# Turning rows in 64-row tiles into pairs of PSUM banks, with the order inside a step written out

## The chip, the cores and the metric

The kernel runs on one core of one Trainium2 chip. The metric is device time of one execution in microseconds. A profile of one execution comes with it: a record of each instruction's start and duration on each engine. The engines are called PE (TensorE, matrix multiply; PEld is its weight load), DVE (VectorE), ACT (ScalarE), POOL (GpSimd) and SP (SyncE, which here only issues DMA transfers). PE writes only to PSUM, a memory of eight banks, each of 512 fp32 values per partition. POOL does not read PSUM here, so what PE writes is taken out by ACT and DVE.

## The reference

Two sequences, of 2048 and 512 rows with 1024 channels, go through the same two layers and a last norm. The change lies in the second layer, Fourier mixing:

```
def fourier_layer(x, g, w_gate, w_out):
    h = rmsnorm(x, g)
    hg = h.astype(jnp.float32).reshape(b, s, N_FGROUPS, FGROUP_CH)
    f = jnp.fft.fftn(hg, axes=(1, 3), norm="ortho").real
    f = f.reshape(b, s, d).astype(x.dtype)
    gate = h @ w_gate
    return x + (f * jax.nn.silu(gate)) @ w_out
```

After it follows `rmsnorm(x, final_norm)`. In words: a transform over channels (in four groups of 256) and over positions, times a SiLU gate, times the output weights, added to the residual, normed.

## The kernel before, in words

All products are done in about fp32 precision from three matmuls each. A value is split into a high part (an ACT copy into the fp32r type) and a low part (a DVE subtraction), and `matmul3` (line 94) multiplies high by high, high by low and low by high. So each operand costs one ACT and one DVE instruction beside the PE work.

The attention layer comes first. It ends about two thirds into the span and is not changed. It already turns 64 rows at a time (line 564): the scores are turned by halves `h` into two banks, `ps[0]` and `ps[1]`, alternating `h` from turn to turn.

The Fourier layer transforms channels and computes gates first (class `Pair`, `gates`). Then come the position transforms. The transform over 2048 positions is split into 16 residues: radix-4 sums on DVE form one or two inputs `g` for each residue `k1`, and `position` multiplies them by a 128x128 cosine and sine table. For each half `hf` of the channels, `A` (cosine part, names `Ap`) and `B` (sine part, names `Bp`) are accumulated by 6 matmuls each. `B` of both halves of one position lies in the two halves of one bank. ACT copies `A` to `u` (lines 1387, 1390), DVE combines it with `B` (lines 1391 to 1394) to the rows `k1` and `16 - k1`, which gives two tiles of 128 rows, and multiplies each by its gate `s2` (line 1397).

The rows of `u` must be turned before the output product, as the channel must lie on the partitions. There are two ways through:

- `step` (residues 0 and 8, then 4, then 2): `position` for new tiles, then `finish` for an older one (48 matmuls into `fo`, the residual added at line 1425, the final norm in `normed`), then the turns of the new tiles in `split_T` (line 1000, 8 turns of 128x128 for each tile, into a new bank for each half), then `finish` of the other older tile. Between the steps DVE makes the inputs of the later residues (lines 1217, 1684 to 1708).
- `Outs` (residues 6, 1, 7, 3, 5): the products of two mirrored tiles share work by sums of their halves. `turn` (line 1442) turns half a tile into a bank, `own` makes the high and low part of a half, `sums` builds the four sums `F` and their parts `S`, and `products` runs seven products of 12 matmuls: `W` with `A[0,0]`, `Z` with `S[1]`, `W` with `S[2]`, `Z` with `S[4]`, `X` with `A[0,1]`, `W` with `S[3]`, `W` with `A[1,1]`. The position transform of the next residue is hooked in between them (`split_g`, `transform`, `turns`), and so are its turns. At the end of `products` the two finished tiles are normed and stored, each by `normed`.

The order of instructions on an engine is chosen by a scheduler when the program is built. It goes by the program's order, by what each instruction needs and by a model of durations. A helper `after(ins, anchor)` adds an edge that only fixes issue order, and `seq(engine, ins)` chains instructions of an engine with such edges. Before the change this is used in the Fourier layer only in few places (the scaling of a norm behind the last combination of `u`, line 1409).

PSUM in this part: three banks `acc` for product accumulators (`psum2`), five banks `bank` (`psum3`) in rotation for `A`, `B` and the turns.

## Time and profile before

| What | Value |
|---|---|
| Runs | 1581.34, 1581.65, 1581.80 us; median 1581.65 us |
| Profiled execution | 1581.36 us, its span 1579.4 us |
| PE busy | 1569.1 us (99%) |
| DVE busy | 1152.7 us (73%) |
| ACT busy | 876.9 us (56%) |
| POOL busy | 446.1 us (28%) |
| TensorE clock granted | 0.999 |

The page's first part lists the busy time of each engine. Matmuls are pipelined: the record of one lasts longer than the distance to the next, so rows of PE overlap, and what a group costs is read from the starts of its neighbours. In the timeline a row is a run of like instructions, with its start, the time from its start to its end, the engine, the line, the output and input names and the count; what ended an idle time before it stands in brackets. A stage view gives, for a stretch of the span, its length and then busy time and number of instructions of PE, PEld, DVE, ACT and POOL. The chain view follows the work that ended last back in time.

### The profile page before, as it was taken

The page shows a single profiled execution, that of the slowest core. Times are in us where ns is not written, and L with a number is a line of the kernel's source. Part 1 is how long each engine was busy: PE and PEld are TensorE (multiplying, and loading weights), DVE is VectorE, ACT ScalarE, POOL GpSimd, SP SyncE. Part 2 cuts the span into 40 slices and gives each one's busy share as a digit, 9 for nine tenths or more (in the row PEclk, how much of TensorE's full clock was granted, in tenths as well). Part 3 has the DMA queues.
Part 4 walks back from the last instruction along what each step waited for, and adds up shares of the span by engine and source line. Part 5 has one row for each costly group of instructions (what it writes and reads, how often), then busy time and mean ns, then how long its engine had stood idle before and what let it go on. Part 6 is the DMA issues. An engine that isn't in the chain of part 4 may idle for free.

```text
span 1579.4 us, 27487 instructions
## 1 busy us (share of the span) xinstructions
PE 1569.1 (99%) x9754; PEld 1321.5 (84%) x9754; DVE 1152.7 (73%) x2793; ACT 876.9 (56%) x2096; POOL 446.1 (28%) x614
## 2 busy tenths in 40 slices
PE   9999999999999999999999999999999999999998
PEld 7888888888888888988888888888888888888886
DVE  6888656877547786378764577669878877989796
ACT  7788535776246784167752476646655554343242
POOL 2575642421404314024222242223112111010110
PEclk9999999999999999999999999999999999999999
DMA  8587695575856567665649556675557569557762
GB/s 302 200 332 283 226 360 210 207 257 202 295 209 222 204 235 272 223 208 220 257 161 334 211 212 227 246 251 204 203 202 259 177 219 407 181 182 299 280 208 80
DMA packets 100996, 373.89 MB, mean 237 GB/s; under 512 B 11267, under 2 KB 22283, under 8 KB 83452
## 3 DMA queue, kind: packets, MB, share of 16 engines
q1 hardware_dynamic: 83148, 298.17, 53.4%
q0 software_dynamic: 16400, 70.04, 11.5%
q10 hardware_dynamic: 1312, 3.94, 0.6%
q8 instruction: 77, 1.26, 0.3%
q14 instruction: 59, 0.48, 0.1%
HBM read 280.84 MB, written 91.26 MB: 236 GB/s over the span
## 4 chain that ended last, share of the span: by engine, by line
PE 95%; DVE 3%; DMA 1%; ACT 1%; issue 1%; POOL 0%; SPq 0%; POOLq 0%; ACTq 0%; DVEq 0%
PE gp L94 14%; PE qp L94 14%; PE spt L94 11%; PE op L94 7%; PE av L590 6%; PE W L94 6%; PE spt L505 6%; PE fo L94 5%; PE vp L94 3%; PE Wo L94 3%; PE Z L94 3%; PE pt L564 3%; PE z L94 2%; PE Zo L94 2%; PE X L94 2%; PE z L1112 1%
## 5 line engine op out<-in xcount | busy, mean ns | idle before, releaser
L94 PE MATMUL gp<-h,wg 128*128 128x512 f32 x960 | 237.8, 396 | 0.0
L94 PE MATMUL qp<-h,wq 128*128 128x512 f32 x960 | 236.9, 395 | 0.0
L524 DVE CUSTOM_DVE_ANT_0 S<-spt,b 128x385 f32<-128x385 f32 (+1 forms) x320 | 156.5, 527 | 105.2 <-PE spt L505 68.0
L94 PEld LDWEIGHTS gp<-h,wg 128*128 128x128 f32 x960 | 174.9, 188 | 37.3 <-issue 1.0
L94 PEld LDWEIGHTS qp<-h,wq 128*128 128x128 f32 x960 | 174.9, 188 | 36.3 <-issue 0.2
L532 ACT ACTIVATE S<-S 128x385 f32<-128x385 f32 (+1 forms) x320 | 188.8, 597 | 19.6 <-DVE S L524 19.3
L572 ACT CAST pts<-pt 128x384 fp32r<-128x384 f32 (+1 forms) x240 | 100.4, 458 | 165.6 <-PE pt L564 156.3
L573 DVE TENSOR_TENSOR pts<-pt,pts 128x384 fp32r<-128x384 f32 (+1 forms) x240 | 114.2, 519 | 23.9 <-ACT pts L572 22.9
L94 PE MATMUL spt<-wo,uT 128*128 128x512 f32 x480 | 120.4, 391 | 0.0
L614 POOL TENSOR_TENSOR uT<-o,uT 128x256 fp32r<-128x256 f32 x75 | 55.5, 740 | 229.6 <-ACT uT L613 224.9
L94 PE MATMUL op<-wo,uT 128*128 128x512 f32 x480 | 118.9, 391 | 0.0
L505 PE MATMUL spt<-kwin,qab 64*128 64x384 f32 (+1 forms) x960 | 118.9, 353 | 0.0
L590 PEld LDWEIGHTS av<-pts,v 128*128 128x128 f32 x576 | 101.4, 188 | 18.8
L94 PE MATMUL fo<-wo,tTu 128*128 128x512 f32 x480 | 115.8, 392 | 0.2 <-ACT wo L1624 0.2
L590 PE MATMUL av<-pts,v 128*128 128x512 f32 (+1 forms) x576 | 115.7, 341 | 0.0
L94 PEld LDWEIGHTS op<-wo,uT 128*128 128x128 f32 x480 | 89.3, 188 | 18.6
L94 PEld LDWEIGHTS spt<-wo,uT 128*128 128x128 f32 x480 | 89.1, 188 | 18.3
L94 PEld LDWEIGHTS fo<-wo,tTu 128*128 128x128 f32 x480 | 88.2, 188 | 17.5 <-ACT wo L1624 0.6
L544 DVE TENSOR_SCALAR S<-S 128x384 f32<-128x384 f32 (+1 forms) x192 | 95.8, 499 | 6.8
L505 PEld LDWEIGHTS spt<-kwin,qab 64*128 64x128 f32 x960 | 74.7, 186 | 28.3 <-issue 26.1
L610 POOL TENSOR_TENSOR o<-o,s 128x256 f32<-128x256 f32 x75 | 55.3, 737 | 134.9 <-DVE o L608 134.5
L564 PEld LDWEIGHTS pt<-ident,S 64*128 64x128 f32 x1328 | 78.4, 138 | 4.2 <-issue 2.1
(333 smaller groups left out, 3195.5 us busy)
## 6 DMA issues: line engine op xcount, KB each, us to landing
wo<-wsd SPq DMA_DIRECT2D x32, 1024.0 KB, 5.2
wq<-wsd SPq DMA_DIRECT2D x31, 1024.0 KB, 7.3
wg<-wsd SPq DMA_DIRECT2D x31, 1024.0 KB, 5.6
x<-x1d SPq DMA_DIRECT2D x40, 512.0 KB, 3.6
b<-b21d SPq DMA_DIRECT2D x40, 512.0 KB, 5.8
b<-rowd SPq DMA_DIRECT2D x40, 384.0 KB, 4.3
xs<-in_x_dram SPq DMA_DIRECT2D x23, 512.0 KB, 6.9
s2d<-gt POOLq DMA_DIRECT2D x40, 256.0 KB, 5.0
```

The costliest lines, as they stand in the source:

```text
L94: pe(PE.matmul(out, a[i], b[j], start=start and i + j == 0, stop=stop and i == 1, skip_group_check=more))
L505: pe(PE.matmul(banks[j][:, 2 + k0 * P : 2 + k1 * P], res["q"][rows, qp, b * P : (b + 1) * P], kwin[g][rows, kp, b * P + k0 * P : b * P + k ...
L524: seq(DVE, DVE.tensor_tensor_reduce(out=s[:, e0:e1], in0=ps[:, 1 + e0 : 1 + e1], in1=st["bias"][:, j, 386 - e1 : 386 - e0][:, ::-1], scale ...
L532: last_exp[0] = seq(ACT, ACT.activation(s[:, e0:e1], s[:, e0:e1], AF.Exp, bias=s[:, 386:387], scale=-1.0, accum_out=s[:, 387:388]))
L544: seq(DVE, DVE.tensor_scalar(s[:, ks], s[:, ks], den, None, ALU.mult))
L564: pe(PE.transpose(ps[h][:, kb, j, :], ss[j][rows, 1 + kb * P : 1 + (kb + 1) * P], ident[rows, rows]))
L572: seq(ACT, ACT.copy(hi, ps[:, k0:k1]))
L573: seq(DVE, DVE.tensor_tensor(lo, ps[:, k0:k1], f32(hi), ALU.subtract))
L590: pe(PE.matmul(to, v, pt, start=n == part == 0, stop=part == 1 and n in (1, len(todo) - 1), skip_group_check=n > 1,))
L610: eng.tensor_tensor(o, o, s, ALU.mult)
L614: low = eng.tensor_tensor(lo, o, f32(hi), ALU.subtract)
L1112: PE.matmul(to, m[part][:, g * P : (g + 1) * P], ch[:, 0, :, odd * P : (odd + 1) * P], start=part == 0, stop=part == 1,)
```

## The change

1. Behind the step for residues 0 and 8 the pool of five banks is closed. A pool with one bank (`one`, for `B`) and a pool with two pairs of banks (`two`) take its place. `A` of one half takes the first bank of a pair, and so do the two accumulators `Vo` at the end of the last products.
2. From then on `half_turns` turns a tile. For each of its 8 blocks of 128 channels it issues two turns of 64 rows, the rows 0 to 63 into the first bank of a pair and the rows 64 to 127 into the second. One pair holds a whole tile. Two tiles take 32 turns in place of 16, chained behind the matmuls of `B` and behind each other. Readers see the pair through a view that puts the halves together again; the mirrored tile is reversed over halves and rows.
3. `step` uses `turned` in place of `split_T`: the same ACT copies and DVE subtractions, half by half over both tiles. The next `finish` starts behind the last turn.
4. `Outs`: `turns` issues all 32 turns at once. `operands` then makes the parts of the first half, sums 1, 2, 3, the parts of sums 1 and 2, and sum 4; `others`, called later, the parts of sum 4, of the two remaining halves and of sum 3. These ACT and DVE instructions are chained in that order.
5. Orders within the products are written out. `Z` with `S[4]` is cut into three quarters behind `A` and the last quarter behind `B`; `X` follows it; the adding of `X` follows the gates; `W` with `S[3]` runs two quarters, then the turns, then the other two. The norm of the first tile is split into its sum and its scaling, with the rest of that product between. The norm of the second tile goes into the next products, between the splits of the two inputs `g` (`late`, `weigh`). The outputs and the plain gate loads are issued behind the last read of `go`.
6. In the last `finish` before the products, the turns of residue 6 come between its two halves.

The diff, cut to its core:

```diff
     def bank(name):
+        if turning:
+            if name[0] == "B":
+                return turning[0].tile([P, 512], F32, tag="one", name=name)
+            return two_banks(name)[:, 0]
         return banks[-1].tile([P, 512], F32, tag="bank", name=name)
+    def two_banks(name):
+        return turning[1].tile([P, 2, 512], F32, tag="two", name=name)
+
+    def half_turns(tiles):
+        views = []
+        for i, src in enumerate(tiles):
+            two = two_banks(f"tw{i}")
+            views.append(two.rearrange("p h (k q) -> p k h q", k=KD))
+            for k in range(KD):
+                for h in range(2):
+                    hp = slice(64 * h, 64 * h + 64)
+                    ins = PE.transpose(two[:, h, 64 * k : 64 * k + 64], src[hp, k * P : (k + 1) * P], ident[hp, hp])
+                    after(seq("turns", ins), chain["B"])
+        return views
...
+            def turned(us):
+                out = [[] for u in us]
+                views = half_turns([u for u, r in us])
+                for hf in range(2):
+                    for (u, r), v, parts in zip(us, views, out):
+                        t = main.tile([P, 2, 512], F32R, align_bytes=LINE, tag="hT", bufs=8, name=f"tTu{r[0]}_{hf}")
+                        src = v[:, 4 * hf : 4 * hf + 4]
+                        if r[2] is not None:
+                            src = src[:, :, ::-1, ::-1]
+                        hi, lo = (quarters(t[:, i]) for i in range(2))
+                        ACT.copy(hi, src)
+                        DVE.tensor_tensor(lo, src, f32(hi), ALU.subtract)
...
-                    acc(a, (cs, ns), 0, 130)
+                    chain["A"] = acc(a, (cs, ns), 0, 130)
-                    acc(b, (sn, cs), P, P)
+                    chain["B"] = acc(b, (sn, cs), P, P)
...
                 def operands(self):
-                    self.turn(0, 0)
+                    self.turns()
                     self.own(0, 0)
-                    self.turn(1, 0)
-                    self.turn(1, 1)
-                    self.sums(1)
-                    self.sums(2)
-                    self.turn(0, 1)
+                    for i in (1, 2, 3):
+                        self.sums(i)
+                    self.halve(1)
+                    self.halve(2)
                     self.sums(4)
+
+                def others(self):
+                    self.halve(4)
                     self.own(0, 1)
-                    self.sums(3)
+                    self.halve(3)
                     self.own(1, 1)
...
-                    prod(Z, S[4], wo[12:16], four, False)
+                    if last:
+                        end = prod(Z, S[4], wo[12:16], four, False)
+                    else:
+                        prod(Z, S[4], wo[12:16], (0, 1, 2), False, chain["A"])
+                        end = prod(Z, S[4], wo[12:16], (3,), False, chain["B"])
                     add(xa, 1, Z)
-                    prod(X, A[0, 1], wo[4:8], four, True)
-                    add(xa, 0, X)
+                    prod(X, A[0, 1], wo[4:8], four, True, end)
+                    whole = add(xa, 0, X)
+                    for ins in gated_by[-2:]:
+                        after(whole, ins)
+                    chain["turns"] = prod(W, S[3], ft["T3"], (0, 1), False)
                     hooks[2]()
+                    def upper():
+                        prod(W, S[3], ft["T3"], (2, 3), False, chain["turns"])
+                        seq("dve", add(xb, 1, W))
                     if not last:
-                        normed(xa, self.us[0][1])
+                        scaled = norm(xa, self.us[0][1], "act", "dve")
+                        upper()
+                        scaled()
+                        hooks[3]()
...
-                    prod(W, S[3], ft["T3"], four, False)
-                    add(xb, 1, W)
                     if not last:
                         prod(W, A[1, 1], ft["N4"], four, False)
-                        add(xb, 0, W)
-                        normed(xb, self.us[1][1])
-                        return
+                        seq("dve", add(xb, 0, W))
+                        return xb, self.us[1][1]
...
+            p3.close()
+            for i in (1, 2):
+                turning.append(es.enter_context(tc.tile_pool(name=f"psum{3 + i}", bufs=i, space=PSUM, reuse_waits="tile")))
             emit(4)
...
-            o.operands()
-            finish(*pend.pop(0))
+            finish(*pend.pop(0), o.operands)
+            o.others()
             o.load()
+            chain["steps"] = True
...
+                    scaled = []
+                    def weigh():
+                        if late[0]:
+                            scaled.append(norm(*late[0], "dve"))
-                    nxt["p"] = [halves_of(name, *gl, 0), None]
+                    nxt["p"] = [halves_of(name, *gl, 0, weigh), None]
+                    for f in scaled:
+                        f()
...
-                o.products((split_g, transform, turns))
+                late[0] = o.products((split_g, transform, turns, lambda: nxt["o"].others()))
```

More of the change, by code (lines that the diff above doesn't have):

```diff
@@ L89, in inv_rms, with matmul3 @@
         return inv
-    def matmul3(out, a, b, start, stop, more=False):
+    def matmul3(out, a, b, start, stop, more=False, behind=None):
         for i, j in ((0, 0), (0, 1), (1, 0)):
-            pe(PE.matmul(out, a[i], b[j], start=start and i + j == 0, stop=stop and i == 1, skip_group_check=more))
+            ins = pe(PE.matmul(out, a[i], b[j], start=start and i + j == 0, stop=stop and i == 1, skip_group_check=more))
+            after(ins, behind)
+        return ins
     def fetch_w(n, name, late=None):
@@ L1122, in fourier_phase, with prod @@
             last_z, last_c = [None], [None]
-            def prod(out, a, b, ks, first):
+            def prod(out, a, b, ks, first, behind=None):
                 for k in ks:
                     cs = slice(k * P, (k + 1) * P)
-                    matmul3(out, (a[0][:, cs], a[1][:, cs]), b[k], first and k == 0, k == 3, not first)
+                    end = matmul3(
+                        out, (a[0][:, cs], a[1][:, cs]), b[k], first and k == 0, k == 3, not first, None if k > ks[0] else behind
+                    )
+                return end
             b21 = []
@@ L1586, in step @@
                 if pend:
-                    finish(*pend.pop(0))
-                new = [(split_T(u, f"u{r[0]}", r[2] is not None), r) for u, r in new]
+                    end = finish(*pend.pop(0))
+                if turning:
+                    chain["turns"] = end
+                    new = turned(new)
+                else:
+                    new = [(split_T(u, f"u{r[0]}", r[2] is not None), r) for u, r in new]
                 for f in pend:
```

119 lines of the change are left out of this document (73 added, 46 removed).

## The prediction, made before the changed kernel was run

> **What bounds the kernel now.** I read the page first: the busy times, the granted clock, and the chain of work that ended last.
>
> ```profile
> span 1579.4 us, 27487 instructions
> PE 1569.1 (99%) x9754; PEld 1321.5 (84%) x9754; DVE 1152.7 (73%) x2793; ACT 876.9 (56%) x2096; POOL 446.1 (28%) x614
> PEclk9999999999999999999999999999999999999999
> PE 95%; DVE 3%; DMA 1%; ACT 1%; issue 1%; POOL 0%; SPq 0%; POOLq 0%; ACTq 0%; DVEq 0%
> ```
>
> PE is busy 99% of the span, carries 95% of the chain and has its full clock, so only PE time or PE waits can move the end. The shares are averages, so the next view is busy time by stage. I cut it at the starts of the groups of 16 turns: two groups in `step`, then one for each set of outputs.
>
> ```profile
> 1390.38:1417.48 27.10, 26.84 (x137) 22.54 (x136) 26.14 (x36) 12.35 (x22) 2.84 (x3) 1.00 0.45 151
> 1417.48:1449.14 31.66, 31.35 (x158) 26.29 (x157) 29.60 (x41) 8.66 (x18) 1.43 (x2) 1.00 0.63 234
> 1499.09:1523.17 24.08, 24.08 (x125) 20.42 (x125) 21.15 (x37) 10.06 (x21) 4.06 (x4) 1.00 0.60 192
> ```
>
> After the length come PE, PEld, DVE, ACT and POOL. The third stage is all PE, with about 3 us of idle DVE. The first two are not: DVE works 26.14 of 27.10 and 29.60 of 31.66 us, and PE has 0.26 and 0.31 us without work.
>
> The chain in order of time shows that behind the last group the PE runs unbroken almost to the end:
>
> ```profile
> 1547.40 1.75 PE tr L1442 x16
> ...
> 1569.89 2.88 PE Vo L94 x24
> 1572.78 0.02 issue
> ```
>
> So what a product step saves reaches the end. What the two early stages save must first pass their DVE.
>
> **The turns.** The changed groups are the two of `step` that begin at 1390.38 and 1417.48, and five of `Outs`: 80 turns in all, that is 5 x 16. The (0, 8) step before them keeps its form.
>
> ```profile
> 1390.38 1.91 PE L1000 MATMUL tru<-ident,up 128*128 128x128 f32 x16
> 1417.48 1.91 PE L1000 MATMUL tru<-ident,up 128*128 128x128 f32 x16
> L1442 PE MATMUL tr<-ident,up 128*128 128x128 f32 x80 | 9.5, 272 | 0.0
> 1498.63 0.62 PE L94 MATMUL Wo<-fT,S 128*128 128x512 f32 x2
> 1499.09 1.91 PE L1442 MATMUL tr<-ident,up 128*128 128x128 f32 x16
> 1500.76 0.71 PE L94 MATMUL Wo<-fT,S 128*128 128x512 f32 x2
> ```
>
> I measure a group from the start of the last matmul ahead of it to the start of the second one behind it, since the pipe refills there. One 512-column matmul is about 0.39 us long in such rows. The one ahead starts at 1498.63 + 0.62 - 0.39 = 1498.86, the second behind at 1500.76 + 0.71 - 0.39 = 1501.08: 2.22 us.
>
> The new form, 64 rows at a time with the two halves alternating, runs already in the attention phase. There are 24 of them between full-array matmuls here:
>
> ```profile
> 606.07 0.61 PE L94 MATMUL spt<-wo,uT 128*128 128x512 f32 x2
> 606.61 0.65 PE L564 MATMUL pt<-ident,S 64*128 64x64 f32 x13
> 607.04 0.22 PE L564 MATMUL spt<-ident,S 64*128 64x64 f32 x1
> 607.10 0.22 PE L564 MATMUL pt<-ident,S 64*128 64x64 f32 x1
> 607.11 0.22 PE L564 MATMUL spt<-ident,S 64*128 64x64 f32 x1
> ...
> 607.36 0.22 PE L564 MATMUL spt<-ident,S 64*128 64x64 f32 x1
> 607.51 0.73 PE L94 MATMUL spt<-wo,uT 128*128 128x512 f32 x2
> ```
>
> The two halves of a pair start 0.01 us apart, and pairs follow at (607.36 - 607.04) / 5 = 0.064 us, call it 0.063. From last ahead (606.07 + 0.61 - 0.39 = 606.29) to second behind (607.51 + 0.73 - 0.39 = 607.85) is 1.56 us for 12 pairs. A group of two tiles has 16 pairs: 1.56 + 4 x 0.063 = 1.81 us. The change replaces 2.22 by 1.81: **0.41 us a group**. That includes the entry into and the exit from the 64-row form, which cost more than with full turns. Seven groups make 2.87 us.
>
> TensorEngine Tiling (Array Packing) of the Trainium skill, section Theoretical Speedup, allows up to twice the rate where the contraction is 64 or less. By that rule alone a group would save half of its 1.67 us from start to start, 0.83, and seven 5.8. I keep the rows, in which entry and exit are paid.
>
> **The two early groups.** Here the stalls of PE decide:
>
> ```profile
> 1405.51 2.68 PE L94 MATMUL fo<-wo,tTu 128*128 128x512 f32 x11
> 1408.44 0.74 PE L94 MATMUL Bp<-gp,tbp 128*128 128x256 f32 x4 [0.26 <-DVE up L1394]
> 1435.77 2.23 PE L94 MATMUL fo<-wo,tTu 128*128 128x512 f32 x9
> 1438.31 0.51 PE L94 MATMUL Ap<-gp,tbp 128*128 128x260 f32 x2 [0.31 <-DVE gp L1357]
> ```
>
> The last `fo` matmul starts at 1405.51 + 2.68 - 0.39 = 1407.80, the next at 1408.44: 0.64, where about 0.23 is usual, so 0.41 lost. The same at 1438.31: 1437.61 to 1438.31, 0.47 lost. Both wait for a DVE that has hardly paused since the group ahead. A PE that arrives 0.41 earlier waits 0.41 longer. I therefore take 0 for these two groups; the bounds are 0 and 0.82, and the other way the 0.88 us of stalls could go too if the DVE came to other places. A loss has the same bound, about 0.9: these stalls can also double, as the order there is not written out.
>
> **The product steps.** The five groups of `Outs` make 5 x 0.41 = 2.05 us, if no new wait takes it. Two things are tight.
>
> First, `B` of the second half writes the bank that the DVE has just read for the first half. The DVE view and the PE view of one step:
>
> ```profile
> 1492.82 0.41 DVE L1394 TENSOR_TENSOR up<-up,Bp 128x254 f32<-128x254 f32 x1
> 1491.73 2.03 PE L94 MATMUL Zo<-wo,S 128*128 128x512 f32 x8
> 1493.59 0.86 PE L94 MATMUL Bp<-gp,tbp 128*128 128x256 f32 x6
> 1497.62 1.22 DVE L1397 TENSOR_TENSOR up<-up,s2p 128x1024 f32<-128x1024 f32 x1
> ```
>
> The DVE is done at 1493.23, `B` starts at 1493.59: 0.36 of slack. PE will come 0.41 earlier after the turns before; the new order lays at least 9 instead of 8 `Z` matmuls between `A` and the end of the `Z` product, which can give 0.23 back. Slack left: 0.36 - 0.41 + 0.23 = 0.18. The turns themselves wait for the second gate, done at 1498.84, 0.25 ahead of 1499.09; the second tile now comes 8 pairs, 0.5 us, behind the first, and `B` still has 21 matmuls behind it before the turns. That wait does not grow.
>
> Second, a pair of banks now holds a whole tile. Today the halves have banks of their own, and ACT and DVE read side by side:
>
> ```profile
> 1475.62 0.59 ACT L1449 CAST tT<-tr 128x512 fp32r<-128x512 f32 x1 [7.35 <-PE tr L1442]
> 1476.10 1.08 ACT L1459 COPY F<-tr 128x512 f32<-128x512 f32 x2
> 1476.23 0.69 DVE L1450 TENSOR_TENSOR tT<-tr,tT 128x512 fp32r<-128x512 f32 x1 [0.90 <-ACT tT L1449]
> ```
>
> If reads of one pair must take turns, the second copy into `F` waits for the first sum. No row shows the price in this layout. The bounds are 0 (the copy has been done before the DVE wants it) and all five ACT reads of a step in line with the DVE, 5 x 0.59 = 2.95 us. The order of the change (sums 1 to 3 together, the halves behind them, the other copies later) puts only one copy between two DVE reads, and the DVE has `own` and sum 1 to do meanwhile. I estimate 0.1 us for it, and 0.05 for the first copy, which waits for 8 pairs (about 0.11 + 7 x 0.063 + 0.22 = 0.77) instead of starting 0.64 behind the first turn. That is 0.15 us of lateness against 0.18 of slack: no cost. Reading through two banks with runs of 64 instead of 512 I count at the same duration; the number of instructions on ACT and DVE is the same.
>
> **The rest moves nothing on the path.** The late norm of the second tile, with its scaling, its POOL power and its output, goes into the next step. The trace has it there already:
>
> ```profile
> 1485.37 0.32 SPq L1340 DMA_DIRECT2D s2p<-s2d  x1
> 1488.23 1.29 DVE L1409 SCALAR_TENSOR_TENSOR x<-x,invf,gfb 128x1024 f32<-128x1024 f32 x1 [0.46 <-POOL invf L88]
> 1489.55 0.34 SPq L1410 DMA_DIRECT2D out_dram<-x  x1
> ```
>
> The scheduler has put the scaling at 1488.23 and its output on SP at 1489.55, behind the gate load at 1485.37. The queue edges to the last read of `go` change nothing while that read is issued ahead of both. On POOL the power stays behind the indirect load. If this cover went, the DVE's 1.29 us would fall into the stretch ahead of `B` and cost up to that. The turns between the two halves of the last `finish` stand 4 matmuls later than now, among the same work: 0. The split of `Z` into three and one, and the edges for `X`, add no instruction.
>
> **The sum.** The profiled execution took 1581.36 us (span 1579.4), 0.29 under the median of the three runs, 1581.65. Turns of the product steps -2.05, early groups 0, waits 0: 1579.31 on the profiled run's scale, 1579.6 on the median's. I forecast 1579.5, 0.13% less. A difference of 0.2%, 3.2 us, is about what a measurement of this kernel can tell from no change.
>
> **The rivals.**
>
> *More than the turns.* The new order also takes away the two early stalls. Speaks for it: DVE has about 1 and 2 us free in those stages, and the stall at 1408.44 stands behind a scaling that could move. Against: no DVE order is written there. -2.87 - 0.88 = -3.75, about 1577.9. That decides for faster.
>
> *The turns do not run in pairs.* Then 32 turns at about 0.11 us, the distance of today's, make 3.5 us instead of 1.67: +1.8 a group. The rows of 607.10 and 607.11 exclude it while the halves lie in different banks, as they do. I give it no chance of its own.
>
> *Given back.* The lateness of the DVE is 0.5 us more than I think, at `B` of each of the four steps that follow a changed group: 4 x (0.65 - 0.18) = 1.9 back, 1581.5, no change.
>
> *Slower: ACT and DVE take turns on the pairs.* The mechanism above at its far end: the ACT reads of a step stand in line with the DVE's, `B` waits for the DVE in four steps, and PE with it. With three of the five reads the DVE is 3 x 0.59 = 1.77 late, so 4 x (1.77 - 0.18) = 6.4 against -2.05: +4.3, about 1586.0; with all five 4 x 2.77 - 2.05 = +9.0. The point from which it is slower than before is 0.18 + 2.05 / 4 = 0.69 us of lateness, and slower by 0.2% 1.5 us. Against it: the third stage above has 3 us of idle DVE, and the pinned order keeps the reads apart. PSUM — Partial Sum Buffer of the Trainium skill, section PSUM bank collisions raise a hardware error, says that two engines must not read the same bank at the same time. By that rule reads on one pair have to be set apart in time, and this rival's mechanism exists; how much of it falls on the path no run here shows.
>
> **How the numbers follow.** Turns alone, 0.55; more than the turns 0.22; given back 0.10; slower 0.13. A tenth of the first reaches past 3.2 us by part of the early groups, so faster by over 0.2% is 0.27, within 0.2% 0.60, slower 0.13. The likeliest case alone spans 1578.4 to 1580.6 (half an early saving more, a microsecond of new waits). The range goes down to 1577.2, below the second case by the rest of PE's small stalls, and up to 1583.0, above the case of gains given back; the slower case is left out, and little below.
>
> **What would show it.** In the trace of the changed kernel: seven groups of 32 turns of 64x64, pairs 0.06 us apart, 1.8 us by the measure above; the steps between groups 23.7 us instead of 24.1; the waits of `B` for the DVE unchanged or under 0.2 us; the stalls of the two early stages 0.4 longer. I am wrong if pairs of turns do not overlap, if a step shows PE idle behind a DVE or ACT read of a pair, if `A` waits for its pair, or if the early stages keep their gain.

## The result, and the profile after

The changed kernel took 1584.14 us (median of 14 runs, 1582.16 to 1586.64). The kernel before, run beside it, took 1581.50 (14 runs). The ratio is 1.0015, 95% interval 1.0008 to 1.0022: 2.6 us slower. That is still within the 0.2% that I had named as no change, but it moved the other way than forecast, and it lies above my range of 1577.2 to 1583.0. The profiled execution took 1584.17 us.

The page after, its span, busy times and clock:

```profile
span 1582.2 us, 27709 instructions
PE 1569.9 (99%) x9866; PEld 1316.8 (83%) x9866; DVE 1150.5 (73%) x2793; ACT 877.4 (55%) x2096; POOL 442.9 (28%) x614
PEclk9999999999999999999999999999999999999999
```

The clock is as before. The span less the busy time of PE was 10.3 us and is 12.3. So PE waits more, at a busy share that still reads 99%. A wait that is over before the record of the matmul ahead ends does not show in these numbers at all; it shows in the starts.

The view by stage says where. Columns are the stretch, its length, then PE, PEld, DVE, ACT and POOL busy. The stretches run from the first changed group of turns to the first product, from there to the second group of turns in the products, over the next three steps, and from the last group to the end. First the kernel before, then the changed one:

```profile
1390.38:1457.26 66.88, 66.31 (x338) 55.83 (x336) 63.10 (x88) 26.73 (x51) 6.68 (x8) 1.00 0.60 221
1457.26:1474.98 17.72, 17.72 (x90) 15.04 (x89) 13.41 (x25) 3.38 (x9) 1.17 (x2) 1.00 0.96 371
1474.98:1547.24 72.26, 72.26 (x373) 61.31 (x373) 63.45 (x109) 30.20 (x63) 11.56 (x11) 1.00 0.61 204
1547.24:1579.40 32.16, 25.52 (x132) 21.53 (x131) 20.11 (x37) 11.34 (x23) 2.20 (x4) 0.97 0.22 82
```

```profile
1390.91:1456.78 65.87, 65.45 (x386) 53.64 (x386) 61.92 (x86) 24.94 (x47) 6.68 (x8) 1.00 0.60 220
1456.78:1476.73 19.95, 18.65 (x91) 15.21 (x89) 14.97 (x26) 5.56 (x13) 2.16 (x3) 1.00 1.01 393
1476.73:1550.24 73.51, 72.81 (x421) 59.26 (x421) 63.20 (x109) 30.57 (x63) 7.47 (x10) 1.00 0.55 187
1550.24:1582.20 31.96, 24.73 (x147) 20.89 (x146) 19.95 (x37) 11.43 (x23) 2.19 (x4) 0.95 0.22 83
```

| Stretch | Before | After | Difference | Forecast |
|---|---|---|---|---|
| up to the first changed group | 1390.38 | 1390.91 | +0.53 | 0 |
| two early groups and the first of the products | 66.88 | 65.87 | -1.01 | -0.41 |
| first products | 17.72 | 19.95 | +2.23 | 0 |
| three product steps | 72.26 | 73.51 | +1.25 | -1.23 |
| last group to the end | 32.16 | 31.96 | -0.20 | -0.41 |

The first line is scatter: nothing is changed there, and in the kernels of this study, all with the same code up to there, the first changed group starts between 1389.68 and 1391.23. The rest adds up to +2.27. Two places made the kernel slower: the first products, once, and every product step, by 0.42 us each where I had forecast 0.41 less.

**The turns themselves.** Timeline rows of PE for one group of the changed kernel:

```profile
1500.23 1.07 PE L119 MATMUL Wo<-fT,S 128*128 128x512 f32 x4
1501.23 1.21 PE L97 MATMUL tw<-ident,up 64*128 64x64 f32 x32
1502.36 1.66 PE L119 MATMUL Wo<-fT,S 128*128 128x512 f32 x6
```

With the prediction's measure, the last ahead starts at 1500.23 + 1.07 - 0.39 = 1500.91. The second behind starts 0.34 after 1502.36, at 1502.70. That is 1.79 us against the forecast 1.81. The turns save PE what they should, and the step is longer all the same.

**A product step.** The step from 1501.23 in the changed kernel, DVE and PE rows that close it:

```profile
1502.60 0.69 DVE L1519 TENSOR_TENSOR tT<-tw,tT 128x512 fp32r<-128x512 f32 x1 [1.11 <-ACT tT L1518]
...
1514.59 1.29 DVE L1468 SCALAR_TENSOR_TENSOR x<-x,invf,gfb 128x1024 f32<-128x1024 f32 x1 [0.45 <-POOL invf L113]
1515.79 0.68 DVE L1565 TENSOR_TENSOR x<-x,Zo 128x512 f32<-128x512 f32 x1
1516.39 1.29 DVE L1408 TENSOR_TENSOR gp<-go,gp 128x512 fp32r<-128x512 f32 x2
```

```profile
1512.78 0.96 PE L119 MATMUL Wo<-fT,S 128*128 128x512 f32 x3 [0.23 <-DVE x L1565]
...
1517.13 1.11 PE L119 MATMUL Ap<-gp,tbp 128*128 128x260 f32 x5
1518.09 2.25 PE L119 MATMUL Zo<-wo,S 128*128 128x512 f32 x9
...
1524.31 1.52 PE L119 MATMUL Wo<-fT,S 128*128 128x512 f32 x6
1525.76 0.96 PE L97 MATMUL tw<-ident,up 64*128 64x64 f32 x24
```

The same rows of the kernel before, in its step from 1499.09:

```profile
1500.34 0.69 DVE L1450 TENSOR_TENSOR tT<-tr,tT 128x512 fp32r<-128x512 f32 x1 [0.91 <-ACT tT L1449]
...
1514.14 1.29 DVE L1357 TENSOR_TENSOR gp<-go,gp 128x512 fp32r<-128x512 f32 x2
```

```profile
1514.93 1.07 PE L94 MATMUL Ap<-gp,tbp 128*128 128x260 f32 x6
1515.83 2.00 PE L94 MATMUL Zo<-wo,S 128*128 128x512 f32 x8
...
1522.03 1.30 PE L94 MATMUL Wo<-fT,S 128*128 128x512 f32 x5
1523.17 1.03 PE L1442 MATMUL tr<-ident,up 128*128 128x128 f32 x8
```

Count from the first turn. Before, the DVE begins on the turned rows at 1.25. It works in one line, with one longer pause (0.47, for POOL), up to the low parts of the second half of `g`. The first is done at 15.74, the second at 16.34 (1514.14 + 1.29). `Z`, which stands behind `A` of that half, starts at 16.74, 0.40 behind the second low part. After, the DVE begins at 1.37, the low parts are done at 15.85 and 16.45, and `Z` starts at 16.86, 0.41 behind. The DVE's line is as long as before, 15.08 us against 15.09; it only starts 0.12 later. So in both kernels `A` of the second half waits for the DVE, which has worked in one line since the turns.

Before, this hardly shows. `A` starts 0.23 behind the last `W`, PE's usual distance. The wait lies among its six matmuls, which take 0.90 up to `Z`, while those of the first half stand 0.12 apart, 0.72 for six. (After, the row has five; the sixth came earlier.) After, PE had 0.41 less turning to do on the way there, and one `W` matmul less (0.23 us from start to start), and yet `A` starts at 15.90 instead of 15.84, 0.06 *later*. PE waited on the way, at `W` with `S[2]` for the DVE's addition (0.52 from the matmul ahead instead of 0.12), and at `A`.

Behind `A` up to the next turns PE runs without a wait in both. From `Z` to the turns it took 7.34 us (1515.83 to 1523.17) and takes 7.67 (1518.09 to 1525.76). One more matmul of `W` with `S[3]` lies ahead of the turns, 6 instead of 5: 0.23. The last `W` is followed by the turns after 0.32 instead of 0.23: 0.09. Together 0.32, with the 0.12 by which the DVE starts later 0.44, and the step is 0.45 longer (24.53 against 24.08). The saved 0.41 lies in the other part, where PE waits for the DVE anyway.

**The first products.** Before and after, the DVE waits here for the residual `x1d` from memory, and adds `W` to it. Rows of the kernel before, and then of the changed one:

```profile
1459.03 0.68 DVE L1357 TENSOR_TENSOR gp<-g1r,gp 128x512 fp32r<-128x512 f32 x1
1459.63 0.68 DVE L1357 TENSOR_TENSOR gp<-g1s,gp 128x512 fp32r<-128x512 f32 x1
1460.23 0.68 DVE L1357 TENSOR_TENSOR gp<-g1r,gp 128x512 fp32r<-128x512 f32 x1
...
1462.48 0.69 DVE L1490 TENSOR_TENSOR x<-x,Wo 128x512 f32<-128x512 f32 x1 [1.50 <-DMA x<-x1d]
```

```profile
1461.83 0.69 DVE L1565 TENSOR_TENSOR x<-x,Wo 128x512 f32<-128x512 f32 x1 [1.93 <-DMA x<-x1d]
1462.43 1.28 DVE L1468 SCALAR_TENSOR_TENSOR x<-x,invf,gfb 128x1024 f32<-128x1024 f32 x1
1463.63 0.68 DVE L1408 TENSOR_TENSOR gp<-g1r,gp 128x512 fp32r<-128x512 f32 x1
...
1464.37 0.63 PE L119 MATMUL Ap<-gp,tbp 128*128 128x260 f32 x3 [1.30 <-DVE gp L1408]
```

The transfer lands no later than before. But before, three of the four low parts of `g` had been made ahead of the wait. After, they are chained behind the addition and a norm's scaling, and `A` waits 1.30 us for the first. By the starts PE loses 1.79 us there and inside `A`. The sixth `W` and the entry into the turns add 0.32; that and a wait of 0.11 ahead of one `W` make up the 2.23.

### The profile page after: what moved, and what is told of

Read it like the earlier page. It is cut to its first block, busy times and chain, and to the rows that moved or that the text cites. A ratio compares the mean times of both kernels' runs of the same rounds, so it can differ in the third digit from the quotient of the medians.

```text
span 1582.2 us, 27709 instructions
## 1 busy us (share of the span) xinstructions
PE 1569.9 (99%) x9866; PEld 1316.8 (83%) x9866; DVE 1150.5 (73%) x2793; ACT 877.4 (55%) x2096; POOL 442.9 (28%) x614
```

## The experiments

My theory after these two traces, called LOOP in the expectations: a product step is closed by a loop from the turns through the DVE to `A`, and through PE back to the turns. (A closure, below, is a place where PE waits for the DVE and so closes such a loop.) What is saved on PE between turns and `A` is lost there, and what is put on PE between `A` and turns is paid in full. Beside it there is a one-time stall in the first products. The rival SHARE: ACT and DVE must take turns on the pairs of banks, and that makes the DVE late. The rival PE: PE's own work is the bound, and no order matters. The kernels change the new kernel, one thing at a time and then together. "Step" below is the distance between the sixth and seventh of the last eight groups of turns (1499.09 to 1523.17 in the kernel before), "first stretch" that between the fourth and fifth (1449.14 to 1474.98). Both come from the starts of the turns in each trace, one execution for each kernel. The kernel before took 1580.94 to 1582.03 us where it ran beside the experiments, so ratios compare better than medians.

| Kernel | Step | First stretch | Median | Ratio to before, 95% |
|---|---|---|---|---|
| before | 24.08 | 25.84 | 1581.50 | |
| changed | 24.53 | 26.67 | 1584.14 | 1.0015 (1.0008 to 1.0022) |
| one `W` quarter | 24.31 | 26.25 | 1583.78 | 1.0008 (0.9999 to 1.0017) |
| `Z` two and two | 24.52 | 27.05 | 1584.07 | 1.0022 (1.0013 to 1.0031) |
| both of these | 24.09 | 27.93 | 1583.03 | 1.0010 (1.0001 to 1.0019) |
| late scaling later | 24.02 | 26.79 | 1582.11 | 1.0001 (0.9992 to 1.0010) |
| first addition later | 24.51 | 25.06 | 1582.63 | 1.0005 (0.9996 to 1.0014) |
| the last two | 24.03 | 25.05 | 1580.81 | 0.9996 (0.9987 to 1.0005) |
| all four | 23.68 | 24.66 | 1579.60 | 0.9989 (0.9980 to 0.9998) |
| all four, again | 23.68 | 24.66 | 1580.11 | 0.9992 (0.9983 to 1.0001) |
| all four, `Z` one and three | 23.96 | 24.76 | 1580.62 | 0.9996 (0.9987 to 1.0005) |
| changed, full turns | 25.05 | 29.94 | 1587.98 | 1.0034 (1.0022 to 1.0046) |
| all four, full turns | 24.24 | 29.74 | 1586.23 | 1.0031 (1.0020 to 1.0042) |
| no written orders | 25.61 | 27.14 | 1587.67 | 1.0042 (1.0028 to 1.0055) |

### The late norm's scaling behind the low parts

The scaling of the late norm (1.29 us on the DVE, and 0.45 of waiting for POOL ahead of it) stands in the loop, just ahead of the low parts that `A` needs. Here it is moved behind them.

```diff
                     nxt["p"] = [halves_of(name, *gl, 0, weigh), None]
-                    for f in scaled:
-                        f()
+                    nxt["scaled"] = scaled
...
                     nxt["p"][1] = halves_of(name, *gl, 1)
+                    for f in nxt["scaled"]:
+                        f()
```

> One edit to the changed kernel: the scaling of the late norm (1.29 us of DVE and the 0.45 us wait for POOL ahead of it) is chained behind the low parts of the second half of g instead of ahead of them. Nothing is left out. LOOP: A of the second half comes earlier, but W with S[2] still waits for the addition of W, which stands ahead of the scaling; the gain ends there: 0.3 to 0.45 us a step, 24.1, about 1 us in all, 1583. Rival PE: no change, 24.5 and 1584. Rival SHARE: the scaling is no PSUM read; no change.

DVE and PE rows of one step, from 1499.69:

```profile
1513.13 1.28 DVE L1408 TENSOR_TENSOR gp<-go,gp 128x512 fp32r<-128x512 f32 x2
1514.33 1.28 DVE L1468 SCALAR_TENSOR_TENSOR x<-x,invf,gfb 128x1024 f32<-128x1024 f32 x1
```

```profile
1515.44 0.78 PE L119 MATMUL Ap<-gp,tbp 128*128 128x260 f32 x5
1516.05 2.23 PE L119 MATMUL Zo<-wo,S 128*128 128x512 f32 x9
```

The low parts come 13.44 behind the first turn instead of 15.16. The five matmuls of `A` take 0.61 up to `Z` instead of 0.96, and start at 15.75. They wait no more. The step is 24.02, 0.5 shorter (I had expected 0.3 to 0.45), at an unchanged amount of work on every engine. That is LOOP: PE alone would have left the step as it was. The wait at `W` with `S[2]` is still there, as expected. The first stretch did not shrink (26.79), as that stall is another one.

### The first addition behind the low parts

```diff
-                    seq("dve", add(xa, 0, W))
+                    first = add(xa, 0, W)
+                    if self.n != 6:
+                        seq("dve", first)
                     hooks[0]()
+                    if self.n == 6:
+                        after(first, chain["dve"])
```

> One edit to the changed kernel: in the first products alone (residue 6) the addition of W, which waits for the load of x, is put behind the low parts of the first half of g instead of ahead of them. Nothing is left out. In the trace of the changed kernel A waits 1.3 us for these low parts, and DVE waits 1.93 us for the load. LOOP with this wait: A no longer waits for the load; the stretch from the first to the second group of turns of the products shortens by 1.5 to 1.8 us and the kernel to about 1582.5; the runs scatter less. Rival: the load is only one of several things late there, W with S[2] waits for the same addition and takes most of it back: under 0.5 us.

The first stretch is 25.06 instead of 26.67, and the steps stay at 24.5. The row of `A` now names no wait at the place of the 1.30 us:

```profile
1461.54 1.22 PE L119 MATMUL Ap<-gp,tbp 128*128 128x260 f32 x6
```

So the stall was the chained order, not the transfer, and it is worth 1.6 us once.

### Both DVE edits together

> The changed kernel with both DVE edits of the runs before: the late norm's scaling behind the low parts of the second half, and the addition of W of the first products behind the low parts. Nothing is left out. LOOP (each step is closed by a loop through the DVE; the first products have a stall of their own): the two gains add, since they lie at different places: product steps 24.03 us, the stretch from 1449 to the next turns about 25.1 instead of 26.7, together -1.6 - 2.0 against the changed kernel: about 0.1% under the kernel before. Rival (the gain of the first products is given back at the next place where PE meets the DVE): steps 24.0 but the kernel not under the time before.

Steps 24.03, first stretch 25.05: each gain is where it was alone. The ratio of 0.9996 can't be told from 1. The kernel is back at the time before; with these two places mended, the new kernel as a whole has gained nothing yet.

### One quarter of `W` ahead of the turns

This takes 3 matmuls, 0.68 us, out of the part between `A` and the turns and puts them behind the turns.

```diff
-                    chain["turns"] = prod(W, S[3], ft["T3"], (0, 1), False)
+                    chain["turns"] = prod(W, S[3], ft["T3"], (0,), False)
...
-                        prod(W, S[3], ft["T3"], (2, 3), False, chain["turns"])
+                        prod(W, S[3], ft["T3"], (1, 2, 3), False, chain["turns"])
```

> One edit to the changed kernel: one quarter (3 matmuls) instead of two of W with S[3] ahead of the turns, three behind them. Nothing is left out. Theory LOOP: a product step is a loop through DVE. From the first turn DVE works through a fixed chain to the low parts of the second half of g, A of that half waits for it, and from there PE runs without a gap back to the next turns; the step of 24.5 us is that loop, not PE's work (about 23.7). Taking 3 matmuls of 0.227 us out of the closing stretch should shorten each of the three steps by up to 0.68 us: 23.8 to 23.9, and the kernel by about 2 us, to about 1582. Rival PE: the step is PE's own work, moving matmuls changes nothing: 24.5, 1584. Rival SHARE: DVE is late because ACT and DVE take turns on a pair of banks; the closing stretch is shorter here too, so this run does not tell it from LOOP, the run with full turns does.

The step came to 24.31, not below 24. It gained 0.22 of 0.68, and the row of the turns says what ended it:

```profile
1501.02 1.21 PE L97 MATMUL tw<-ident,up 64*128 64x64 f32 x32 [0.42 <-DVE up L1451]
...
1517.87 2.22 PE L119 MATMUL Zo<-wo,S 128*128 128x512 f32 x9
```

`Z` starts 16.85 behind the first turn, against 16.86 in the changed kernel, though three `W` matmuls more lie on the way there. So work that PE does between the turns and `A` costs nothing here, as LOOP has it. But the turns now wait for the last gate. There is a second closure: `B` of the second half, then the DVE's combinations and the two gates, then the turns.

### `Z` cut two and two, alone and with one quarter of `W`

```diff
-                        prod(Z, S[4], wo[12:16], (0, 1, 2), False, chain["A"])
-                        end = prod(Z, S[4], wo[12:16], (3,), False, chain["B"])
+                        prod(Z, S[4], wo[12:16], (0, 1), False, chain["A"])
+                        end = prod(Z, S[4], wo[12:16], (2, 3), False, chain["B"])
```

> The changed kernel with one edit: Z cut two and two quarters instead of three and one, so that at least 6 instead of 9 Z matmuls lie between A and B of the second half. Nothing is left out. LOOP, second closure: B starts 0.4 to 0.45 us earlier (at 18.4 to 18.5 us behind the first turn instead of 18.94, then the bank's read at 17.95 + 0.41 is what it waits for), and combinations, gates and turns follow: steps 24.1 us instead of 24.5. Rival (the three Z quarters cover a wait that A makes, and B's place costs nothing): steps 24.5.

> The changed kernel with one W quarter ahead of B's stretch for the turns instead of two, and Z cut two and two, so that B stands after two quarters of Z instead of three. Nothing is left out. LOOP with a second closure (B, then the DVE's combinations and gates, then the turns): with one quarter alone a step took 24.31 us and the turns came right behind the last gate. B can now start as soon as the DVE has read the bank, about 0.45 us earlier; gates and turns follow: steps 24.0 us. Rival (the turns do not wait for this chain): steps stay at 24.3.

Alone it changed nothing: 24.52, where I had expected 24.1. `A` stands where it stood and PE is full from there to the turns, so the order of its work in between is free. I had counted the ninth `Z` matmul ahead of `B` as lost time; it is not. What counts is the sum of the work, as the decomposition above now has it. Together with one quarter, where the second closure binds, the same cut took the step from 24.31 to 24.09, and the wait of the turns for the gate from 0.42 to 0.20. The first stretch of that kernel is 27.93, 1.3 longer than in the changed kernel. Its trace shows why: the granted clock was 0.79 from 1463 to 1466 us and 0.64 from 1466 to 1469, where the changed kernel has 1.00, and `W` matmuls there start 0.43 apart instead of 0.23.

### All four

> The changed kernel with all four edits: scaling of the late norm behind the low parts, addition of W of the first products behind the low parts, one W quarter, Z cut two and two. Nothing is left out. LOOP: both closures are loosened, so that PE is nearly the bound: its own work in a step is 24.08 - 0.41 = 23.67 us; steps 23.65 to 23.85 us, first products' stretch about 25.0; kernel 1578.5 to 1579.5, 0.15 to 0.2% under the kernel before. Rival (a third place holds the steps at 24.0): about 1580.4.

> The same kernel as in the run with all four edits, timed again: steps 23.65 to 23.7 us but for the first at 24.0; 0.1 to 0.15% under the kernel before. Nothing is left out.

Rows of one step's end, from the first:

```profile
1514.70 0.78 PE L119 MATMUL Ap<-gp,tbp 128*128 128x260 f32 x5
1515.31 1.55 PE L119 MATMUL Zo<-wo,S 128*128 128x512 f32 x6
1516.70 0.62 PE L119 MATMUL Wo<-fT,S 128*128 128x512 f32 x2
1517.15 0.88 PE L119 MATMUL Bp<-gp,tbp 128*128 128x256 f32 x6
...
1521.97 0.39 PE L119 MATMUL Wo<-fT,S 128*128 128x512 f32 x1
1522.56 0.65 PE L97 MATMUL tw<-ident,up 64*128 64x64 f32 x14 [0.20 <-DVE up L1451]
```

Step 23.68: 24.08 less 0.40. That is what the prediction had for the steps, but the agreement is in part chance: the 0.20 at the turns is a wait that the kernel before didn't have, and the small waits at `A` are gone in its place. The first of the three steps took 24.02 in one run and 23.72 in the other; in the longer one PE lost 0.33 among the matmuls of the first half of `A` and `B`, in the other 0.07. The kernel took 1579.60 and 1580.11 us, ratios 0.9989 (0.9980 to 0.9998) and 0.9992 (0.9983 to 1.0001). It is the fastest of this study, by about 0.1%, and one of the two intervals includes 1. Against my expected 1578.5 to 1579.5 it is slightly slower. Its rows name no wait of PE in the step but one, 0.20 at the turns.

### All four, with `Z` one and three

That last wait should go if `B` comes earlier still.

```diff
-                        prod(Z, S[4], wo[12:16], (0, 1), False, chain["A"])
-                        end = prod(Z, S[4], wo[12:16], (2, 3), False, chain["B"])
+                        prod(Z, S[4], wo[12:16], (0,), False, chain["A"])
+                        end = prod(Z, S[4], wo[12:16], (1, 2, 3), False, chain["B"])
```

> The kernel with all four edits, with Z cut one and three quarters instead of two and two, so that B of the second half stands 3 Z matmuls earlier still. Nothing is left out. With all four edits a step took 23.68 us, and the one place where PE loses more than its usual pause is ahead of the turns, 0.585 us from the last W instead of the 0.319 of the changed kernel: 0.27 us. LOOP: that is the second closure (B, combinations, gates, turns), B starts up to 0.45 earlier, the 0.27 goes, and a step is what PE has to do, 23.4 us; about 1 us under the four edits' kernel, 1578.5 to 1579. Rival (0.585 is what the entry into the turns takes here, PE is the bound): steps stay at 23.68.

```profile
1498.19 1.20 PE L97 MATMUL tw<-ident,up 64*128 64x64 f32 x32
...
1514.61 0.86 PE L119 MATMUL Zo<-wo,S 128*128 128x512 f32 x3
1515.76 0.74 PE L119 MATMUL Wo<-fT,S 128*128 128x512 f32 x2 [0.29 <-DVE x L1565]
1516.34 0.88 PE L119 MATMUL Bp<-gp,tbp 128*128 128x256 f32 x6
```

The wait ahead of the turns is gone, as LOOP had it. But the step is 23.96, longer by 0.28. Two `W` matmuls that the scheduler lays ahead of `B` now come too early: they wait for the DVE to have added the last `W`. From the last `Z` (1514.61 + 0.86 - 0.39 = 1515.08) to the first `W` there are 0.68 us instead of 0.23. A wait of 0.45 took the place of one of 0.27. The kernel took 1580.62 us, ratio 0.9996, where I had expected 1578.5 to 1579. An order with `B` ahead of these two matmuls wasn't tried.

### Full turns in the new order, without and with the four edits

```diff
-            views.append(two.rearrange("p h (k q) -> p k h q", k=KD))
+            views.append(two.rearrange("p b (k h q) -> p (b k) h q", k=4, h=2))
             for k in range(KD):
-                for h in range(2):
-                    hp = slice(64 * h, 64 * h + 64)
-                    ins = PE.transpose(two[:, h, 64 * k : 64 * k + 64], src[hp, k * P : (k + 1) * P], ident[hp, hp])
-                    after(seq("turns", ins), chain["B"])
+                ins = PE.transpose(two[:, k // 4, (k % 4) * P : (k % 4 + 1) * P], src[:, k * P : (k + 1) * P], ident)
+                after(seq("turns", ins), chain["B"])
```

> One edit to the changed kernel: the turns are full 128x128 ones again, a bank of the pair for each half of a tile, so that each half has a bank of its own; every order is kept. Nothing is left out. PE's work grows by 0.41 us for each of seven groups. LOOP: DVE can begin 0.1 us sooner after the first turn and the stretch behind is the same: the steps stay at 24.4 to 24.5 and the kernel at 1584, within 1 us, though PE does 2.9 us more. Rival PE: 24.9 a step and 1587. Rival SHARE: with a bank for each half ACT and DVE no longer take turns, DVE catches up and the step goes back to 24.1 or less, 1583 or less.

> The kernel with all four edits, but turned by 16 full 128x128 turns, a bank for each half of a tile, in the places of the 64-row turns. Nothing is left out. LOOP: with both closures loose PE is the bound, so a step costs what PE has to do: 23.67 + 0.41 = 24.08 us; steps 24.05 to 24.3 (the DVE starts 0.3 to 0.6 later behind the slower turns, which the loosened chain may not hide whole). So the turns' 0.41 us are worth nothing in the changed kernel and all of it here. Rival (the four edits alone made the gain): steps stay at 23.7.

In the changed kernel full turns made the step 25.05, 0.52 longer, where I had expected 24.4 to 24.5. The forecasts of the rival PE, 24.9 and 1587, are nearer to the measured 25.05 and 1587.98. The rows decide. DVE and PE behind the turns at 1504.12:

```profile
1505.81 0.69 DVE L1517 TENSOR_TENSOR tT<-tw,tT 128x512 fp32r<-128x512 f32 x1 [1.33 <-ACT tT L1516]
1506.69 1.41 DVE L1534 TENSOR_TENSOR F<-F,tw 128x512 f32<-128x512 f32 x2 [0.18 <-ACT F L1527]
...
1516.27 0.97 PE L117 MATMUL Wo<-fT,S 128*128 128x512 f32 x3 [0.34 <-DVE x L1563]
1521.58 2.25 PE L117 MATMUL Zo<-wo,S 128*128 128x512 f32 x9
```

The DVE starts at 1.69 instead of 1.37, and on the sums at 2.57 instead of 1.98. `A` follows at 16.51 instead of 15.90, and `Z` at 17.46 instead of 16.86, 0.60 later. PE still waits on the way, 0.34 at `W` instead of 0.23. So PE's work is not the bound here either, and the nearness of that forecast is chance. What I had wrong is the DVE's start: the turns do lie in the loop, by the time at which the second tile's halves are complete, but not by the time they take on PE.

With the four edits, full turns cost 0.56 (24.24 against 23.68), and the same closure at the turns binds in both (they wait 0.20 and 0.16 for the gate). So with the written orders the 64-row turns are worth 0.52 and 0.56 a step; that they would be worth nothing in the changed kernel was wrong. Read the other way, the new layout and orders with full turns make a step 0.97 longer than in the kernel before (25.05 against 24.08), and the 64-row turns give 0.52 of it back. Against the kernel before the turns bring the DVE no gain in time: there it had its first half tile at 1.25, now at 1.37.

SHARE is not tested by this run. ACT's second copy into `F` waits for the DVE with a bank for each half as well (0.76). What speaks against SHARE is the DVE's line of 15.08 us, which is no longer than before, and the changed kernel's own rows. ACT does wait for the DVE on a pair, once:

```profile
1503.92 0.59 ACT L1529 COPY F<-tw 128x512 f32<-128x512 f32 x1 [0.85 <-DVE F L1536]
```

But the DVE has its sums to do meanwhile and does not pause for that copy. The first stretches of these two kernels (29.94 and 29.74) hold a longer wait for `x1d`, 3.8 and 4.1 us, and a granted clock of 0.54 and 0.53 from 1466 to 1469. In both, SP issues three loads of `x1d` together, where every other kernel issues two at that place. So their total times say nothing about turns.

### None of the written orders

All edges that fix an order within the steps are left out: `seq` by name returns the instruction unchained, and the `behind` of `Z`, `X`, `W` and the turns, the edges of the gates and of `last_read` are dropped. The scheduler alone decides.

```diff
     def seq(engine, ins):
+        if isinstance(engine, str):
+            return ins
...
-                    after(seq("turns", ins), chain["B"])
...
-                        prod(Z, S[4], wo[12:16], (0, 1, 2), False, chain["A"])
-                        end = prod(Z, S[4], wo[12:16], (3,), False, chain["B"])
+                        prod(Z, S[4], wo[12:16], (0, 1, 2), False)
+                        end = prod(Z, S[4], wo[12:16], (3,), False)
```

> The changed kernel's 64-row turns and pairs of banks, with none of the written orders within a step: the scheduler alone sets the order. Nothing is left out. LOOP (the turns' time stands in a loop through the DVE, whatever the order): steps 24.0 to 24.5 us. Rival (the written orders are what costs, the turns alone save their 0.41): steps 23.7 us, kernel about 1579.5.

Steps of 24.85, 25.61 and 26.11: longer than either theory had. The scheduler lays the late scaling ahead of the parts of the first half, and PE waits for those:

```profile
1505.67 1.66 PE L119 MATMUL Wo<-wo,tT 128*128 128x512 f32 x6 [1.28 <-DVE tT L1519]
```

So the written orders as a whole save time with this layout. Details of them cost: the place of the late scaling, the chained addition in the first products, and the second quarter of `W` ahead of the turns.

## Why the prediction was wrong

**What bounds the kernel.** I concluded that only PE time or PE waits can move the end, and the waits decided it. But I took "PE busy 24.08 of 24.08" for a PE bound, and it was balanced: in the kernel before already, `A` of the second half ran close behind the low parts that it needs, at the end of a DVE line of 15 us, and lost 0.18 to them inside rows that read as busy. I had looked for slack at `B` and at the gate, and never at `A` of the second half. The idle DVE time that I counted as room (3 us a step) lies mostly ahead of that line and behind it: 0.91 at the turns and 1.30 at `B`.

**The turns, 0.41 a group.** Right: 1.79 us measured against 1.81. The rule of the Trainium skill that I weighed (TensorEngine Tiling (Array Packing), section Theoretical Speedup) would by my estimate have made it 0.83. The pairs follow at 0.06 where full turns follow at 0.11, a little over half, and entry and exit took the rest. By the same page, section Key Properties, a change of the tiling mode drains the engine, and the trace fits that: 0.32 us from the last `W` to the first turn instead of 0.23.

**Early groups, 0.** Wrong on the careful side: with the first group of the products they kept 1.01 of their 1.23 us. The stalls there moved but did not grow by what PE saved: PE was without work for 0.57 us of that stretch and is for 0.42. So the early stages kept most of their gain, which I had named as a sign of being wrong.

**Product steps, 5 x 0.41, "if no new wait takes it".** This is the step that failed. Three full steps came out 1.25 us longer instead of 1.23 shorter. The wait that took the saving did not have to be new: an old one, at `A`, takes what PE saves ahead of it unless the DVE starts earlier too, and the DVE started 0.12 later. What made the steps longer than before is that 0.12, the sixth `W` (0.23) and the entry into the turns (0.09). That the loop through `A` is the closure is shown by two runs: the scaling moved (24.02), and three `W` matmuls more ahead of `A` with `Z` unmoved (16.85).

**The slack of 0.18 at `B` against 0.15 of lateness.** The lateness was sized well: the DVE starts 0.12 later. But the slack that met it was not that of `B`, which grew: `B` of the step shown starts 0.58 behind the DVE's last read of its bank, 0.33 before. The ninth `Z` matmul gives nothing back on the path, as the cut of `Z` alone showed. And the sixth `W` matmul ahead of the turns I did not count at all, as it adds no work; it costs its 0.23 in every step. That the wait for the second gate does not grow held for the changed kernel; it becomes the next closure as soon as `W` is taken from ahead of the turns.

**"The rest moves nothing on the path".** Wrong in the first products: the written DVE order put the addition that waits for memory ahead of the low parts, worth 1.6 us. I had named what a lost cover of the scaling would cost ahead of `B`, and not looked at what else was chained. For the product steps the trace of before had the scaling in the same place, as I said; but it stands on the loop, and moving it in the changed kernel is worth 0.5. The same move in the kernel before wasn't tried.

**The end.** The last group's 0.41 reached the end by half: -0.20. Where the rest went I have not followed up.

**The rivals.** "Given back", at 1581.5, has the right engine, but the wrong wait, and it stopped at the time before. "ACT and DVE take turns", at 1586.0, has the right direction and is nearer to the measured 1584.14, but by luck: its mechanism cost nothing. By PSUM — Partial Sum Buffer of the Trainium skill, section PSUM bank collisions raise a hardware error, reads of one bank must be set apart. The row of the 0.85 us wait does not contradict that, but the same copy waits 0.76 with a bank for each half, so it does not show it. Either way it is ACT time that nobody waits for. "More than the turns" did not come. The four edits bring the kernel to where the main forecast was, 1579.60 and 1580.11 against 1579.5, but by orders that the forecast did not have.

## What to carry to other kernels

A repeating step can be closed by a loop over engines, and then a saving counts only where it shortens that loop. Take one period, count every engine from the same point, and look at each place where an instruction of the busiest engine starts within 0.1 us of what it needs; in this kernel that engine's busy share, 24.08 of 24.08, did not show it. Where orders are written out, move what waits for memory, and what nobody in the loop needs, behind what the next engine waits for.

## What was not expected of the hardware

The entry into and the exit from the 64-row form cost what they cost in the attention phase, but seen alone they are large beside the turns: 0.32 us ahead, 0.15 from the last turn to the next matmul, and 0.34 from that one to the second, where two full matmuls stand 0.23 apart. The 32 turns between take 0.99 (1.21 less the 0.22 that one lasts), 0.06 for a pair. Between kernels with the same code in front, the chain up to the first changed group shifts by up to 1.55 us (1389.68 to 1391.23), more than half of what this change moved.

The clock fell in the first products in three of the fourteen traces, to the 0.64, 0.54 and 0.53 above. Each time PE had just waited, 1.29, 1.82 and 1.84 us by its rows; but the changed kernel waits 1.30 at the same place and kept 1.00. What decides is not shown.
